# Where a split weight is split: the sums of the second MLP matrix stored whole and split at their use

## Chip, cores and metric

The kernel runs on one core of one Trainium2 chip. The metric is the device time of one execution in microseconds (us), as the median of several runs. A second source is one profiled execution, whose trace gives every instruction of the five engines (TensorE: PE, with its weight loads PEld; VectorE: DVE; ScalarE: ACT; GpSimd: POOL; SyncE: SP, which issues nearly all DMAs here).

## The reference, cut to what matters

One layer of a hybrid decoder over 2048 prompt positions and 8 x 4 sampled ones, in float32, with D_MODEL 1024 and D_FF 4096. Two mixers (a gated linear recurrence and a chunked state-space scan) read one projection, and an MLP follows:

```python
x = x + jnp.concatenate([y_lru, y_ssd], axis=-1) @ w_out
m = rmsnorm(x, g_mlp)
x = x + jnp.square(jax.nn.relu(m @ w_up)) @ w_down
```

`w_up` is 1024 x 4096 and is called the first matrix here, `w_down` is 4096 x 1024 and is called the second.

## The kernel before

**Split products.** The matmuls take operands of the type float32r. Each operand is split into a high part (a copy into float32r, by ACT) and a low part (the operand minus its high part, by DVE), and each product is three matmuls: high x high, high x low, low x high. In the mixers `mm3` (L233 to L235) does that with weights that `load_w` loads (L218) and splits (ACT L220, DVE L222). In the MLP `product` (L832) does it for one block product.

**Fewer block products.** The MLP multiplies 2 x 2 blocks with seven products instead of eight (a Strassen-like scheme). For that it needs sums and differences of weight blocks: seven for each pair of blocks. They depend on the weights alone, so they are prepared once, while the mixers run, by 64 jobs. Job by job the steps are: `job_load` (eight loads of 64 KB, L1128), `job_first` and `job_second` (four DVE additions, L1133 to L1139), `job_higher` (the ACT copy into high parts, tile jh, L1143), `job_lower` and `job_store` (two DVE subtractions, L1146, and two stores to DRAM, of the high parts, L1150, and of the low parts, L1155). The function `tick` is called at set points of the mixers and runs the next step when enough "time" has been counted. Half of the 64 jobs are for the first matrix (they fill the tensors `up0` to `up15`), half for the second (`dn0` to `dn31`). The tiles jt and jh have one buffer each.

**The MLP.** `mlp` goes over three token parts (348, 346 and 346 columns in each half of the token block) and, in each, over eight slices of D_FF (`NQ`). A slice has two `up` phases, of seven products with four pairs of operands each (12 matmuls), and one `down` phase: four groups of output blocks (g), with seven products of two pairs (6 matmuls) each. In the code a weight load of the first matrix serves one product, one of the second serves two (the fourth load of a group serves one). A weight tile `mw` of 128 x 1024 holds high and low parts; there are six. DVE adds each down product from PSUM into the output tiles x2 (or into a sum u), L951, and ACT and DVE prepare operands and splits (L839 and L840, tiles mhh, mhl, ahh, ahl). At the start five weight loads of the first matrix are issued ahead of the token loads (`ahead`).

**What sets the order.** The framework arranges the instructions of each engine at build time, so that the order on an engine isn't quite that of the code; at run time each engine takes its instructions in the order built, and waits for a semaphore where one isn't ready. A DMA waits on SyncE until its target buffer is free.

Of the kernel before, what the change touches and what calls it, by code (L numbers as in the profile page):

```python
# [16 lines left out]
D = 1024  # L17
# [17 lines left out]
MLP = [(0, 348), (696, 346), (1388, 346)]  # L35
MH, FQ = 348, 4
# [3 lines left out]
TF = (1.0, 1.0, 1.05)  # L40
# [2 lines left out]
X2N = ("m", "y", "xdt", "xdd", "hT")  # L43
XTN = ("xdt", "xdd", "hT")
HS, HR = 2, 4


@with_exitstack
def hymba_step(ctx: ExitStack, tc: tile.TileContext,
# [6 lines left out]
    nc = tc.nc  # L56
    V, S, G, T = nc.vector, nc.scalar, nc.gpsimd, nc.tensor
# [94 lines left out]
    r0 = col["cw_s"]  # L152
# [72 lines left out]
    def mm3(ps, w, m, ops, P, b):  # L225

        h, lo = w
        c0, n = P.blocks[b]
        if isinstance(ops[0], list):
            ops, c0 = ops[b], 0  # L230
        nk = len(ops)
        for k, (xh, xl) in enumerate(ops):
            T.matmul(ps[:m, :n], h[:, k, :m], xh[:, c0:c0 + n], start=k == 0, stop=False)  # L233
            T.matmul(ps[:m, :n], h[:, k, :m], xl[:, c0:c0 + n], start=False, stop=False)  # L234
            T.matmul(ps[:m, :n], lo[:, k, :m], xh[:, c0:c0 + n], start=False, stop=k == nk - 1)  # L235

    gwi = [0]
# [566 lines left out]
    def mlp(residual):  # L804
# [6 lines left out]
        ahead = []  # L811

        def bank():
            return ps8.tile([128, 512], F32, tag="mb", name="mb")

        def tmp(name):
            return mp.tile([128, MH], F32, tag="t", name=name, bufs=16)

        def weights(src, op, m):
            if src is up_d[0] and ahead:  # L820
                return ahead.pop(0)
            w = mp.tile([128, 2, 512], F32R, tag="mw", name="mw", bufs=6)
            nc.sync.dma_start(w[:, :, :m].bitcast(F32), src[:, op])
            return w

        def product(ps, w, ops, n, start):

            nk = len(ops)
            for k, (xh, xl) in enumerate(ops):
                c = slice(128 * k, 128 * k + 128)  # L830
                for i, (wi, x) in enumerate(((0, xh), (0, xl), (1, xh))):
                    T.matmul(ps[:, :n], w[:, wi, c], x[:, :n], start=start and k == 0 and i == 0,  # L832
                             stop=k == nk - 1 and i == 2, skip_group_check=not start)

        def halves(t, n, tag, bufs):
# [66 lines left out]

        def up(q, u, mh, n, fill=()):

            src = up_d[2 * q + u]
            x, y, z, w = bank(), bank(), bank(), bank()
            product(x, weights(src, 0, 512), mh[0], n, True)
            after(0, fill)
            p1 = tmp("p1")
            S.activation(p1[:, :n], x[:, :n], AF.Copy)  # L910
            product(y, weights(src, 1, 512), mh[1], n, True)
            after(1, fill)
            v = tmp("v")
            V.tensor_sub(v[:, :n], p1[:, :n], y[:, :n])
            product(z, weights(src, 2, 512), mh[2], n, True)
            after(2, fill)
            p5 = tmp("p5")
            S.activation(p5[:, :n], z[:, :n], AF.Copy)
            product(w, weights(src, 3, 512), mh[3], n, True)
# [4 lines left out]
            product(x, weights(src, 4, 512), mh[4], n, False)  # L924
            after(4, fill)
            c11 = tmp("c11")
            S.activation(c11[:, :n], x[:, :n], AF.Relu)
            product(z, weights(src, 5, 512), mh[5], n, False)
# [3 lines left out]
            product(w, weights(src, 6, 512), mh[6], n, False)  # L932
            after(6, fill)
            c21 = tmp("c21")
            V.tensor_sub(c21[:, :n], w[:, :n], v[:, :n])
            for c in (c22, c12, c21):
                S.activation(c[:, :n], c[:, :n], AF.Relu)  # L937
            for c in (c11, c12, c21, c22):
                S.activation(c[:, :n], c[:, :n], AF.Square)
            return operands((c11, c12, c21, c22), n, "ah", 29)  # L940

        def down(q, act, x2, us, c0, n, steps):
            for g in range(4):
                if steps:
                    steps.pop(0)()
                src = dn_d[4 * q + g]
                hi, lo = x2[g], x2[g + 4]
                c11, c12, c21, c22 = hi[:, :n], hi[:, n:2 * n], lo[:, :n], lo[:, n:2 * n]

                def add(c, ps, op=ALU.add):  # L950
                    V.tensor_tensor(out=c, in0=c, in1=ps[:, :n], op=op)  # L951

                x, y, z, w = bank(), bank(), bank(), bank()
                ws = {}

                def prod(i, ps, start):
                    if i % 2 == 0:
                        t = mp.tile([128, 2, 512], F32R, tag="mw", name="mw", bufs=6)
                        m = min(2, 7 - i)
                        tv = t.rearrange("p a (b c) -> p (a b c)", c=256)[:, :m * 512]  # L960
                        nc.sync.dma_start(tv.bitcast(F32).rearrange("p (o c) -> p o c", c=512),
                                          src[:, i:i + m].rearrange("p o h c -> p o (h c)"))
                        ws[0] = t.rearrange("p a (b c) -> p a b c", c=256)
                    product(ps, ws[0][:, i % 2], [a[i] for a in act], n, start)
# [12 lines left out]
                prod(2, z, True)  # L977
                add(c22, z, ALU.subtract)
                prod(3, w, True)
                add(c22, w)  # L980
                prod(4, x, False)
                add(c11, x)
                prod(5, z, False)
                add(c12, z)
                prod(6, w, False)
                add(c21, w)
                if q == NQ - 1:
                    V.tensor_add(c12, c12, u)
                    V.tensor_sub(c21, c21, u)
                    V.tensor_sub(c22, c22, u)  # L990
# [120 lines left out]
    dn_d = [dr.tile([128, 7, 2, 256], F32, name=f"dn{j}") for j in range(4 * NQ)]  # L1111
    jobs = []
    for q in range(NQ):
        for u in range(2):
            for k in range(2):
                jobs.append((w_up, FF, 256 * k, 512, [128 * (FQ * q + u + 2 * i) for i in range(2)],
                             up_d[2 * q + u][:, :, :, 256 * k:256 * k + 256]))
        for g in range(4):
            jobs.append((w_down, D, 128 * FQ * q, 256, [128 * (g + 4 * i) for i in range(2)], dn_d[4 * q + g][:, :, :, :]))
    jt, jh = {}, {}  # L1120
    clock = [0, 0.0, 0]
    def job_load(j):

        src, ld, r0, dr_, cols, _ = jobs[j]
        t = jt[j] = wp.tile([128, 7, 256], F32, tag="jt", name="jt", bufs=1)
        for at, i, r in ((0, 0, 0), (3, 1, 0), (4, 0, 1), (6, 1, 1)):
            for k in range(2):
                nc.sync.dma_start(t[:, at, 128 * k:128 * k + 128],  # L1128
                                  dap(src, (r0 + dr_ * r + 128 * k) * ld + cols[i], [[ld, 128], [1, 128]]))
# [6 lines left out]
    def job_second(j):  # L1136
        t = jt[j]
        V.tensor_add(t[:, 1], t[:, 2], t[:, 0])
        V.tensor_add(t[:, 5], t[:, 4], t[:, 1])  # L1139

    def job_higher(j):
        h = jh[j] = wp.tile([128, 7, 256], F32R, tag="jh", name="jh", bufs=1)
# [226 lines left out]
```

## Time and profile before

| | |
|---|---|
| runs, median (lowest to highest of 3) | 3085.63 us (3080.34 to 3088.36) |
| the profiled execution | 3082.9 us, span 3081.2 us |
| mean granted TensorE clock | 0.97 |
| mixers | 0 to about 1724 us |
| MLP | about 1724 to 3081 us |
| DMA: moved, mean rate | 708.99 MB, 230 GB/s |
| last job step of the second matrix | DVE L1146 at 1682.0 us, store L1155 at 1683.0 us |

Rows of groups give line, engine, operation, what it writes and reads, the count, then busy us and mean ns of one, then the idle time of the engine before them and who ended it. A row of a wait gives who waited, for whom, us in total, times and the longest. A row of a timeline gives start, length and, in square brackets, the idle time before it and who ended it. A row of the chain that ended last gives start, length and what ran, or which DMA was on its way.

### The profile page before, as it was taken

The numbers are of one execution on the slowest core, as the hardware profiler recorded it, in microseconds if no ns is written. First come the engines' busy times: TensorE is split into PE (matmuls) and PEld (weight loads), VectorE is DVE, ScalarE is ACT, GpSimd is POOL, SyncE is SP. The second block draws the span as 40 slices with busy tenths as digits, with TensorE's granted clock in tenths as the row PEclk, the third lists the DMA queues.
The fourth block names the chain that finished last, engine by engine and source line by source line (L and its number), as shares of the span: only waits on it lengthen the run. The fifth ranks groups of instructions, "written<-read, shape, count | busy, mean of one in ns | idle before, by whom it ended". The sixth has DMA issues, their size and how long they took to land.

```text
span 3081.2 us, 49470 instructions
## 1 busy us (share of the span) xinstructions
PE 2888.0 (94%) x18150; PEld 2789.5 (91%) x18150; DVE 2168.8 (70%) x4422; ACT 1390.9 (45%) x2580; POOL 171.1 (6%) x270
## 2 busy tenths in 40 slices
PE   6999998989999898899989699999999999999997
PEld 6999897888988887899989599999999999999997
DVE  6888788688777878888787645556845556654556
ACT  5553685354357845444883323233432223432322
POOL 0000120010001300000120000000000000000000
PEclk9999998999999998999999799999999999999999
DMA  5555556766665577666656888888988888988885
GB/s 177 156 186 162 165 178 198 236 199 185 205 192 177 179 239 228 184 195 189 194 183 222 277 289 267 281 277 272 319 280 271 284 267 280 318 265 281 268 276 202
DMA packets 534481, 708.99 MB, mean 230 GB/s; under 512 B 44421, under 2 KB 414265, under 8 KB 534240
## 3 DMA queue, kind: packets, MB, share of 16 engines
q1 hardware_dynamic: 534016, 705.56, 71.8%
q8 instruction: 144, 2.36, 0.3%
q0 software_dynamic: 224, 0.27, 0.1%
q14 instruction: 97, 0.79, 0.1%
HBM read 541.43 MB, written 164.27 MB: 229 GB/s over the span
## 4 chain that ended last, share of the span: by engine, by line
PE 47%; DVE 8%; DMA 5%; ACT 4%; issue 1%; SPq 1%; POOL 0%; DVEq 0%; ACTq 0%
PE mb L832 39%; PE mm L235 2%; PE mm L233 2%; PE mm L234 2%; DVE jt L1146 1%; SPq L1128 1%; DMA dn<-jt 1%; DMA up<-jt 1%; DMA mb<-mn_d 1%; DMA mw<-dn 1%; DMA m<-cum 1%; DVE u L412 1%; DVE yt L1027 1%; DVE th L794 0%; ACT jh L1143 0%
## 5 line engine op out<-in xcount | busy, mean ns | idle before, releaser
L233 PE MATMUL mm<-xh,wh 128*128 128x384 f32 (+3 forms) x2160 | 712.6, 331 | 31.8 <-ACT xe L399 14.5
L235 PE MATMUL mm<-xh,wl 128*128 128x384 f32 (+3 forms) x2160 | 705.8, 328 | 3.9 <-DVE wl L222 3.8
L234 PE MATMUL mm<-xl,wh 128*128 128x384 f32 (+3 forms) x2160 | 705.4, 327 | 0.1
L832 PE MATMUL mb<-mhh,mw 128*128 128x346 f32 (+1 forms) x2688 | 655.2, 323 | 17.2 <-ACT mhh L839 16.6
L832 PE MATMUL mb<-ahh,mw 128*128 128x346 f32 (+1 forms) x2688 | 652.5, 323 | 13.1 <-DVE x L951 4.4
L832 PEld LDWEIGHTS mb<-mhh,mw 128*128 128x128 f32 x2688 | 475.8, 191 | 19.4 <-ACT mhh L839 18.3
L832 PEld LDWEIGHTS mb<-ahh,mw 128*128 128x128 f32 x2688 | 470.7, 189 | 19.6 <-ACT ahh L839 5.7
L233 PEld LDWEIGHTS mm<-xh,wh 128*128 128x128 f32 (+1 forms) x2160 | 409.0, 190 | 47.4 <-ACT xe L399 17.5
L832 PE MATMUL mb<-mhl,mw 128*128 128x346 f32 (+1 forms) x1344 | 437.3, 326 | 1.4 <-DVE mhl L840 1.4
L832 PE MATMUL mb<-ahl,mw 128*128 128x346 f32 (+1 forms) x1344 | 434.1, 323 | 0.4 <-DVE ahl L840 0.2
L235 PEld LDWEIGHTS mm<-xh,wl 128*128 128x128 f32 (+1 forms) x2160 | 408.2, 189 | 13.0 <-DVE wl L222 6.5
L234 PEld LDWEIGHTS mm<-xl,wh 128*128 128x128 f32 (+1 forms) x2160 | 409.0, 189 | 3.8 <-issue 1.0
L951 DVE TENSOR_TENSOR x<-x,mb 128x346 f32<-128x346 f32 (+1 forms) x480 | 244.5, 514 | 144.4 <-PE mb L832 143.1
L220 ACT ACTIVATE wh<-raw 128x1024 fp32r<-128x1024 f32 (+1 forms) x159 | 165.4, 1042 | 241.0 <-PE mm L234 181.0
L832 PEld LDWEIGHTS mb<-mhl,mw 128*128 128x128 f32 x1344 | 255.0, 190 | 2.8 <-DVE mhl L840 2.6
L832 PEld LDWEIGHTS mb<-ahl,mw 128*128 128x128 f32 x1344 | 253.7, 189 | 1.4 <-DVE ahl L840 1.4
L910 ACT ACTIVATE p<-mb 128x346 f32<-128x346 f32 (+1 forms) x48 | 21.9, 457 | 473.0 <-PE mb L832 470.9
L222 DVE TENSOR_TENSOR wl<-raw,wh 128x1024 fp32r<-128x1024 f32 (+1 forms) x159 | 190.7, 1201 | 20.5 <-ACT wh L220 19.4
L412 DVE SCALAR_TENSOR_TENSOR u<-xe,prm,u 128x768 f32<-128x768 f32 (+2 forms) x180 | 169.9, 944 | 16.6 <-ACT u L410 14.6
L233 PE MATMUL mm<-nh,wh 128*128 128x384 f32 (+2 forms) x384 | 131.2, 342 | 30.8 <-DVE x L446 27.8
L937 ACT ACTIVATE c<-c 128x346 f32<-128x346 f32 (+1 forms) x144 | 71.3, 495 | 192.5 <-DVE c L923 114.6
L1146 DVE TENSOR_TENSOR jt<-jt,jh 128x1024 fp32r<-128x1024 f32 (+1 forms) x128 | 137.9, 1094 | 25.0 <-ACT jh L1143 24.8
(305 smaller groups left out, 4218.6 us busy)
## 6 DMA issues: line engine op xcount, KB each, us to landing
mw<-up SPq DMA_DIRECT2D x336, 512.0 KB
mw<-dn SPq DMA_DIRECT2D x288, 512.0 KB
raw<-in_w_in_dram SPq DMA_DIRECT2D x108, 512.0 KB
up<-jh SPq DMA_DIRECT2D x32, 896.0 KB
up<-jt SPq DMA_DIRECT2D x32, 896.0 KB
dn<-jh SPq DMA_DIRECT2D x32, 896.0 KB
dn<-jt SPq DMA_DIRECT2D x32, 896.0 KB
raw<-in_w_out_dram SPq DMA_DIRECT2D x48, 512.0 KB
```

Of the source, the lines that this page charges most:

```text
L220: S.activation(h, raw, AF.Copy)
L222: V.tensor_tensor(out=lo, in0=raw, in1=h.bitcast(F32), op=ALU.subtract)
L233: T.matmul(ps[:m, :n], h[:, k, :m], xh[:, c0:c0 + n], start=k == 0, stop=False)
L234: T.matmul(ps[:m, :n], h[:, k, :m], xl[:, c0:c0 + n], start=False, stop=False)
L235: T.matmul(ps[:m, :n], lo[:, k, :m], xh[:, c0:c0 + n], start=False, stop=k == nk - 1)
L412: V.scalar_tensor_tensor(out=u[:, :W], in0=xe[:, k:k + W], scalar=pc(wn, k * nt + j), in1=u[:, :W], op0=ALU.mult, op1=ALU.add)
L832: T.matmul(ps[:, :n], w[:, wi, c], x[:, :n], start=start and k == 0 and i == 0, stop=k == nk - 1 and i == 2, skip_group_check=not start)
L937: S.activation(c[:, :n], c[:, :n], AF.Relu)
L951: V.tensor_tensor(out=c, in0=c, in1=ps[:, :n], op=op)
L1027: V.scalar_tensor_tensor(out=yt[:m], in0=src[:m], scalar=rs[:m, i:i + 1], in1=gfb[:m, 512 * hf:512 * hf + 512], op0=ALU.mult, op1=ALU.mult)
L1128: nc.sync.dma_start(t[:, at, 128 * k:128 * k + 128], dap(src, (r0 + dr_ * r + 128 * k) * ld + cols[i], [[ld, 128], [1, 128]]))
L1146: V.tensor_tensor(out=jt[j][:, a:b].bitcast(F32R), in0=jt[j][:, a:b], in1=jh[j][:, a:b].bitcast(F32), op=ALU.subtract)
```

## The change

The jobs of the second matrix end after the sums: one step, `job_whole`, stores the seven sums whole (128 x 1792 float32), and the split moves into the MLP. There a load of the second matrix brings sums of two products (128 x 512, or 128 x 256) into a tile `mr` of two buffers (`NR`), ACT copies the high part into `mw`, and DVE subtracts into its second half. `mw` has five buffers instead of six. The loads of both matrices are asked for in the order of their use by `ask`, up to two ahead (`NA`), and `prepare` splits up to two ahead (`NP`). At the start two loads are ahead of the token loads instead of five. In `mm3` the matmuls with low parts of weights come behind all matmuls with high parts. The steps of the jobs are 320 instead of 384, and `tick` counts slower in the same ratio. With `UPJ` false and `DNJ` true the first matrix is still split in the mixers.

```diff
+UPJ, DNJ = False, True
+NR, NM, NA, NP = 2, 5, 2, 2
...
 def mm3(ps, w, m, ops, P, b):
...
             T.matmul(ps[:m, :n], h[:, k, :m], xl[:, c0:c0 + n], start=False, stop=False)
+
+        for k, (xh, xl) in enumerate(ops):
             T.matmul(ps[:m, :n], lo[:, k, :m], xh[:, c0:c0 + n], start=False, stop=k == nk - 1)
...
-        def weights(src, op, m):
-            if src is up_d[0] and ahead:
-                return ahead.pop(0)
-            w = mp.tile([128, 2, 512], F32R, tag="mw", name="mw", bufs=6)
-            nc.sync.dma_start(w[:, :, :m].bitcast(F32), src[:, op])
-            return w
+        def raw_weights(src, m):
+            t = mp.tile([128, 512], F32, tag="mr", name="mr", bufs=NR)
+            nc.sync.dma_start(t[:, :m], src)
+            return t
+
+        def parts_of(t, m):
+            w = mp.tile([128, 2, 512], F32R, tag="mw", name="mw", bufs=NM)
+            S.activation(w[:, 0, :m], t[:, :m], AF.Copy)
+            V.tensor_sub(w[:, 1, :m], t[:, :m], w[:, 0, :m].bitcast(F32))
+            return w
...
+        def ask():
...
+                m = min(2, 7 - i)
+                if DNJ:
+                    asked.append((raw_weights(src[:, i:i + m].rearrange("p o c -> p (o c)"), 256 * m), 256 * m))
...
+        def prepare():
+            if asked:
+                t, m = asked.pop(0)
+                ready.append(parts_of(t, m) if m else t)
+
+        def weights():
+            while len(asked) < NA:
+                n = len(asked)
+                ask()
+                if len(asked) == n:
+                    break
+            while len(ready) < NP and asked:
+                prepare()
+            return ready.pop(0)
...
-        ahead.extend([weights(up_d[0], op, 512) for op in range(5)])
+        while len(asked) < NA:
+            ask()
+        while len(ready) < NP - 1:
+            prepare()
...
+    def job_whole(j):
+
+        nc.sync.dma_start(jobs[j][5], jt[j])
+        del jt[j]
...
-    stages = (job_load, job_first, job_second, job_higher, job_lower, job_store)
+    steps_ = [(st, j) for j in range(len(jobs)) for st in
+              (job_load, job_first, job_second) + ((job_higher, job_lower, job_store) if jobs[j][6] else (job_whole,))]
```

**The order, first place: DVE in a down phase.** The second slice of the first token part, from the end of its first group on. Before, DVE has the last operand split and then only additions from PSUM (u: into the running sum; x: into the output tiles):

```order
L840 TENSOR_TENSOR ahl<-t_18790,ahh 128x348
L951 TENSOR_TENSOR x_18243<-x_18243,mb 128x348 x2
L951 TENSOR_TENSOR x_18247<-x_18247,mb 128x348
L951 TENSOR_TENSOR u<-u,mb 128x348 x2
L951 TENSOR_TENSOR x_18248<-x_18248,mb 128x348 x2
L951 TENSOR_TENSOR x_18244<-x_18244,mb 128x348 x2
L951 TENSOR_TENSOR x_18248<-x_18248,mb 128x348
```

Now, at the same place (L902 is the operand split, L1014 the addition, L830 the new subtraction of a weight):

```order
L902 TENSOR_TENSOR ahl<-t_18685,ahh 128x348
L1014 TENSOR_TENSOR x_18090<-x_18090,mb 128x348
L830 TENSOR_TENSOR mw<-mr,mw 128x512
L1014 TENSOR_TENSOR x_18094<-x_18094,mb 128x348
L1014 TENSOR_TENSOR u<-u,mb 128x348
L830 TENSOR_TENSOR mw<-mr,mw 128x512
L1014 TENSOR_TENSOR u<-u,mb 128x348
L1014 TENSOR_TENSOR x_18095<-x_18095,mb 128x348
L1014 TENSOR_TENSOR x_18091<-x_18091,mb 128x348
L1014 TENSOR_TENSOR x_18095<-x_18095,mb 128x348
L830 TENSOR_TENSOR mw<-mr,mw 128x256
```

The subtractions of loads 5, 6 and 7 of the phase (counted from 0) now stand between the additions, each behind additions that themselves wait for TensorE.

**Second place: PE at the start of the third group of the same phase.** The names are mb (the PSUM bank), ah..h and ah..l (high and low part of an operand) and mw (the weight tile). Before, product by product:

```order
L832 MATMUL mb_18945<-ahh_18635,mw_18949 128x348
L832 MATMUL mb_18945<-ahl_18636,mw_18949 128x348
L832 MATMUL mb_18945<-ahh_18635,mw_18949 128x348
L832 MATMUL mb_18945<-ahh_18795,mw_18949 128x348
L832 MATMUL mb_18945<-ahl_18796,mw_18949 128x348
L832 MATMUL mb_18945<-ahh_18795,mw_18949 128x348
L832 MATMUL mb_18946<-ahh_18639,mw_18949 128x348
```

Now:

```order
L894 MATMUL mb_18864<-ahh_18527,mw_18854 128x348
L894 MATMUL mb_18864<-ahl_18528,mw_18854 128x348
L894 MATMUL mb_18865<-ahh_18531,mw_18854 128x348
L894 MATMUL mb_18865<-ahl_18532,mw_18854 128x348
L894 MATMUL mb_18864<-ahh_18527,mw_18854 128x348
L894 MATMUL mb_18864<-ahh_18690,mw_18854 128x348
L894 MATMUL mb_18864<-ahl_18691,mw_18854 128x348
L894 MATMUL mb_18864<-ahh_18690,mw_18854 128x348
```

The four matmuls that need only the weight's high part, of both products of the load, have moved ahead of the first one that needs the low part (the fifth row).

**Third place: SyncE around the second slice.** Before, loads of `mw` follow each other, each of both parts:

```order
L823 DMA mw<-up_144 128x1024 x7
L823 DMA mw<-up_145 128x1024 x7
L961 DMA mw<-dn_162 128x1024 x3
L961 DMA mw<-dn_162 128x512
L961 DMA mw<-dn_163 128x1024 x3
```

Now the loads of the second matrix go to `mr`, at half the size:

```order
L862 DMA mw<-up_144 128x1024 x7
L862 DMA mw<-up_145 128x1024 x6
L824 DMA mr<-dn_162 128x512
L862 DMA mw<-up_145 128x1024
L824 DMA mr<-dn_162 128x512 x2
L824 DMA mr<-dn_162 128x256
L824 DMA mr<-dn_163 128x512 x3
```

The first load of the phase has moved ahead of the last one of the up phase, and the third waits for a buffer that only a subtraction on DVE frees.

More of the change, by code (lines that the diff above doesn't have):

```diff
@@ new lines, in parts_of, with whole_weights, order @@
+        def parts_of(t, m):
+            w = mp.tile([128, 2, 512], F32R, tag="mw", name="mw", bufs=NM)
+            S.activation(w[:, 0, :m], t[:, :m], AF.Copy)
+            V.tensor_sub(w[:, 1, :m], t[:, :m], w[:, 0, :m].bitcast(F32))
+            return w
+        def whole_weights(src):
+            w = mp.tile([128, 2, 512], F32R, tag="mw", name="mw", bufs=NM)
+            tv = w.rearrange("p a c -> p (a c)")
+            return w, tv
+        def order():
+            for _ in MLP:
+                for q in range(NQ):
+                    for u in range(2):
+                        for op in range(7):
+                            yield ("u", up_d[2 * q + u], op)
+                    for g in range(4):
+                        for i in range(0, 7, 2):
+                            yield ("d", dn_d[4 * q + g], i)
@@ new lines, in mlp @@
+        todo = order()
+        asked, ready = [], []
+        def ask():
+            e = next(todo, None)
+            if e is None:
+                return
+            kind, src, i = e
+            if kind == "u":
+                if UPJ:
+                    asked.append((raw_weights(src[:, i], 512), 512))
+                else:
+                    w, tv = whole_weights(src)
+                    nc.sync.dma_start(w.bitcast(F32), src[:, i])
+                    asked.append((w, 0))
+            else:
+                m = min(2, 7 - i)
+                if DNJ:
+                    asked.append((raw_weights(src[:, i:i + m].rearrange("p o c -> p (o c)"), 256 * m), 256 * m))
+                else:
+                    w, tv = whole_weights(src)
+                    nc.sync.dma_start(tv[:, :m * 512].bitcast(F32).rearrange("p (o c) -> p o c", c=512),
+                                      src[:, i:i + m].rearrange("p o h c -> p o (h c)"))
+                    asked.append((w, 0))
@@ L903, in up, with upw @@
         def up(q, u, mh, n, fill=()):
-            src = up_d[2 * q + u]
+            def upw(t):
+                return lambda wi, k: t[:, wi, 128 * k:128 * k + 128]
             x, y, z, w = bank(), bank(), bank(), bank()
-            product(x, weights(src, 0, 512), mh[0], n, True)
+            product(x, upw(weights()), mh[0], n, True)
             after(0, fill)
@@ L910, in up @@
             S.activation(p1[:, :n], x[:, :n], AF.Copy)
-            product(y, weights(src, 1, 512), mh[1], n, True)
+            product(y, upw(weights()), mh[1], n, True)
             after(1, fill)
@@ L914, in up @@
             V.tensor_sub(v[:, :n], p1[:, :n], y[:, :n])
-            product(z, weights(src, 2, 512), mh[2], n, True)
+            product(z, upw(weights()), mh[2], n, True)
             after(2, fill)
@@ L918, in up @@
             S.activation(p5[:, :n], z[:, :n], AF.Copy)
-            product(w, weights(src, 3, 512), mh[3], n, True)
+            product(w, upw(weights()), mh[3], n, True)
             after(3, fill)
@@ L923, in up @@
             V.tensor_sub(c22[:, :n], c22[:, :n], p5[:, :n])
-            product(x, weights(src, 4, 512), mh[4], n, False)
+            product(x, upw(weights()), mh[4], n, False)
             after(4, fill)
@@ L927, in up @@
             S.activation(c11[:, :n], x[:, :n], AF.Relu)
-            product(z, weights(src, 5, 512), mh[5], n, False)
+            product(z, upw(weights()), mh[5], n, False)
             after(5, fill)
@@ L931, in up @@
             V.tensor_add(c12[:, :n], v[:, :n], z[:, :n])
-            product(w, weights(src, 6, 512), mh[6], n, False)
+            product(w, upw(weights()), mh[6], n, False)
             after(6, fill)
@@ L957, in prod @@
                     if i % 2 == 0:
[L958 to L964, printed above, removed]
+                        ws[0] = weights()
+                    t, h = ws[0], i % 2
+                    if DNJ:
+                        at = lambda wi, k: t[:, wi, 256 * h + 128 * k:256 * h + 128 * k + 128]
+                    else:
+                        at = lambda wi, k: t[:, h, 256 * wi + 128 * k:256 * wi + 128 * k + 128]
+                    product(ps, at, [a[i] for a in act], n, start)
                 if q == 0:
@@ L1110, in hymba_step @@
     up_d = [dr.tile([128, 7, 2, 512], F32, name=f"up{j}") for j in range(2 * NQ)]
-    dn_d = [dr.tile([128, 7, 2, 256], F32, name=f"dn{j}") for j in range(4 * NQ)]
+    dn_d = [dr.tile([128, 7, 256], F32, name=f"dn{j}") for j in range(4 * NQ)]
     jobs = []
@@ L1156, in job_store @@
         del jt[j], jh[j]
-    stages = (job_load, job_first, job_second, job_higher, job_lower, job_store)
+    steps_ = [(st, j) for j in range(len(jobs)) for st in
+              (job_load, job_first, job_second) + ((job_higher, job_lower, job_store) if jobs[j][6] else (job_whole,))]
     def tick(w):
-        n = len(stages)
-        clock[1] += w * TF[clock[2]]
-        while clock[1] >= 1 and clock[0] < n * len(jobs):
+        clock[1] += w * TF[clock[2]] * len(steps_) / 384
+        while clock[1] >= 1 and clock[0] < len(steps_):
             clock[1] -= 1
-            j, st = divmod(clock[0], n)
-            stages[st](j)
+            st, j = steps_[clock[0]]
+            st(j)
             clock[0] += 1
```

13 lines of the change are left out of this document (5 added, 8 removed).

## The prediction

> **What bounds the kernel now.** First the page: span, busy shares and slices.
>
> ```profile
> span 3081.2 us, 49470 instructions
> PE 2888.0 (94%) x18150; PEld 2789.5 (91%) x18150; DVE 2168.8 (70%) x4422; ACT 1390.9 (45%) x2580; POOL 171.1 (6%) x270
> ```
>
> Then busy time by stage: the mixers up to 1724 us, the MLP behind them.
>
> ```profile
> 0.00:1724.00 1724.00, 1567.02 (x9942) 1482.70 (x9942) 1374.73 (x2615) 957.21 (x1573) 166.05 (x269) 0.96 0.63 193
> 1724.00:3081.00 1357.00, 1320.94 (x8208) 1306.75 (x8208) 794.08 (x1807) 433.71 (x1008) 5.04 (x1) 0.99 0.84 278
> ```
>
> The columns are length, PE, PEld, DVE, ACT, POOL, granted clock, DMA share, GB/s. In the MLP PE has 36 us idle of 1357 (97% busy) at clock 0.99, DVE works 59% and ACT 32%. In the mixers PE has 157 us idle, with DVE at 80%. So the MLP is bound by TensorE, and anything that delays it there is paid in full; the mixers are a mesh of PE, DVE, ACT and DMA, where freed work pays in part. Next, what PE waits for, in the MLP (first two rows, from 1740 to 3055 us) and in the mixers.
>
> ```profile
> PE mb L832 <- DVE x L951: 4.4, 2, 2.5
> PE mb L832 <- DMA mw<-dn: 4.3, 4, 1.9
> ...
> PE mm L233 <- DVE x L446: 30.1, 14, 5.3
> PE mm L235 <- DVE wl L222: 8.2, 9, 1.7
> ```
>
> Split weights arrive in time now: 4.3 us of waiting for 384 loads of the second matrix. The queue of SyncE says why: its loads wait for a free buffer, so they are issued as early as six buffers allow.
>
> ```profile
> SPq L961 <- PE mb L832: 498.1, 363, 5.2
> ```
>
> **Mixers: what is removed.** Of 64 jobs 32 lose their split: one ACT copy, two DVE subtractions, and one of two stores.
>
> ```profile
> L1146 DVE TENSOR_TENSOR jt<-jt,jh 128x1024 fp32r<-128x1024 f32 x64 | 78.1, 1220 | 25.0 <-ACT jh L1143 24.8
> L1146 DVE TENSOR_TENSOR jt<-jt,jh 128x768 fp32r<-128x768 f32 x64 | 61.9, 967 | 0.0
> L1143 ACT ACTIVATE jh<-jt 128x1792 fp32r<-128x1792 f32 x64 | 108.6, 1697 | 98.8 <-DVE jt L1139 74.5 <-DMA raw<-in_w_out_dram 22.5 <-issue 1.4
> ```
>
> That is 32 x (1.220 + 0.967) = 70 us of DVE and 32 x 1.697 = 54 us of ACT. What of it lies on the path is told by the chain that ended last; in the mixers it is followed from 1038 to 1724 us (686 us).
>
> ```profile
> by line: PE mm L235 10.1%; PE mm L233 10.0%; PE mm L234 9.8%; issue 4.7%; DVE jt L1146 4.0%; SPq L1128 4.0%; DMA dn<-jt 3.2%; DMA up<-jt 3.1%; DMA m<-cum 2.7%; DVE u L412 2.5%; DVE th L794 2.2%; ACT jh L1143 2.2%; DVE wl L222 1.9%; DVE mn L
> ```
>
> L1146 and L1143 have 6.2% of 686 us = 42.5 us; half belongs to the second matrix, 21 us, and over the whole 1724 us that is 21 x 1724/686 = 53 us. A chain that loses a link is soon replaced by the next one, so the bounds are 0 and -53 us; I take the middle, -27. The dropped store widens the better end: dn<-jt has 3.2% (22 us, 55 scaled), and half of that, 28, may go, so -81. The job steps are fewer (320 instead of 384), but the ticks are stretched in the same ratio and the end of the mixers is not set by them: cost 0.
>
> **Mixers: the low parts of weights last.** In mm3 each low part is used after all high parts, so wl is due two thirds of the product later. PE's 8.2 us for wl should go: -8, bounds 0 (the next input is late instead) and -8.2.
>
> **MLP start.** Two weight loads are issued ahead of the token loads instead of five.
>
> ```profile
> 1716.44 7.15 DMA mb<-mn_d
> ```
>
> The first tokens landed 7.15 us after their issue, behind 2.5 MB of weights. Three loads of 512 KB fewer at 278 GB/s are 5.6 us; the third load is then due behind the tokens, so I take -3 (bounds 0 and -5.6).
>
> **MLP: what is added.** Each of the 24 down phases (3 token parts x 8 slices of FF) uses 16 weight loads: per group of output blocks three with two products and one with one. Each now lands as sums of 512 columns (256 for the fourth), is copied by ACT and then subtracted by DVE. Prices lie between neighbouring sizes:
>
> ```profile
> L951 DVE TENSOR_TENSOR x<-x,mb 128x346 f32<-128x346 f32 x320 | 163.0, 514 | 97.4 <-PE mb L832 96.5 <-DMA mw<-dn 0.4
> L222 DVE TENSOR_TENSOR wl<-raw,wh 128x1024 fp32r<-128x1024 f32 x156 | 189.9, 1218 | 20.5 <-ACT wh L220 19.4
> L839 ACT ACTIVATE ahh<-t 128x346 fp32r<-128x346 f32 x128 | 57.7, 486 | 5.1 <-DVE t L848 5.0
> L220 ACT ACTIVATE wh<-raw 128x1024 fp32r<-128x1024 f32 x156 | 164.5, 1056 | 221.5 <-PE mm L234 174.7 <-issue 24.1 <-DVE jt L1138 7.3
> ```
>
> At 512 columns DVE takes 0.514 + 166/678 x 0.704 = 0.69 us and ACT 0.486 + 166/678 x 0.570 = 0.63; at 256, 0.42 and 0.41. With 288 and 96 loads that is 239 us of DVE and 221 us of ACT. By sums there is room: one down phase now shows
>
> ```profile
> 1812.70:1839.50 26.80, 26.80 (x171) 26.69 (x170) 18.25 (x38) 3.42 (x8) 0.00 (x0) 1.00 0.84 273
> ```
>
> 18.25 us of DVE in 26.8, and some 8 us more still fit (four splits are made ahead, in the up phase). The cost comes from order and latency. The raw tiles have two buffers, so a load is issued only when DVE has subtracted the load two before it. This is DVE now, at the start of a down phase:
>
> ```profile
> 1812.77 0.52 DVE L935 TENSOR_TENSOR c<-mb,v 128x348 f32<-128x348 f32 x1 [1.17 <-PE mb L832]
> ...
> 1819.32 0.93 DVE L951 TENSOR_TENSOR x<-x,mb 128x348 f32<-128x348 f32 x2
> 1820.65 0.52 DVE L951 TENSOR_TENSOR x<-x,mb 128x348 f32<-128x348 f32 x1 [0.40 <-PE mb L832]
> ...
> 1823.34 0.52 DVE L951 TENSOR_TENSOR x<-x,mb 128x348 f32<-128x348 f32 x1 [0.44 <-PE mb L832]
> 1824.30 0.52 DVE L951 TENSOR_TENSOR x<-x,mb 128x348 f32<-128x348 f32 x1 [0.44 <-PE mb L832]
> ```
>
> Seventeen operations run back to back from 1812.77 to 1820.25, 0.44 us each (a backlog of the up phase); after that one addition comes with each product, 0.955 us apart. So a group of seven products takes 6.67 us, and load 14 (third of the last group) is due at 3 x 6.67 + 4 x 0.955 = 23.8 us; TensorE does its four high-part products first, so the low part is due at 24.5. In the new order the splits of loads 4, 5 and 6 stand inside the backlog; 19 other operations and three subtractions (0.65 as pitch) end at 19 x 0.44 + 3 x 0.65 = 10.3 us. From load 6 to load 14 the same buffer turns four times. One turn is landing time L + copy 0.63 + subtraction 0.69 + about 0.1 of hand-offs + half an addition in DVE's way, 0.25: L + 1.7. So TensorE is late by 10.3 + 4(L + 1.7) - 24.5 = 4L - 7.4 us in each phase.
>
> L, for 256 KB from issue, stands in no row. The neighbours, sizes first, then the chain's pieces with start and length:
>
> ```profile
> raw<-in_w_out_dram SPq DMA_DIRECT2D x48, 512.0 KB
> gwr<-in_w_a_dram SPq DMA_DIRECT2D x48, 16.0 KB
> ...
> 1528.34 1.91 DMA gwr<-in_w_a_dram
> 1143.46 3.31 DMA raw<-in_w_out_dram
> 1237.98 4.16 DMA raw<-in_w_in_dram
> 2207.32 6.33 DMA mw<-dn
> ```
>
> 16 KB took 1.91 us, 512 KB 3.31 to 4.16 in the mixers and 6.33 in the MLP, where six deep loads queue. With two loads outstanding and half the bytes the quiet rows are nearest: between 1.91 and 3.31, 256 KB gives 2.6. Then 4 x 2.6 - 7.4 = 3.0 us, times 24 = 72 us. Upper end, L = 3.3: 5.8 x 24 = 139. Lower end: the order pins the split of a group's first load behind the last addition of the group before (0.05 + 0.43 + 0.69 = 1.17 us after the due time, 0.64 of it covered by high-part products) at two group boundaries, 1.06 x 24 = 25 us however fast loads land. Behind the waiting subtraction DVE holds the additions, and TensorE needs those before it can reuse a bank, so nothing overtakes. Up weights now have five buffers instead of six and queue behind the raw loads on SyncE; their cover is four products of 1.9 us. At the two seams between token parts, where PE already waits 4.3 us, I add +4 (bounds 0 and +13).
>
> **Sum.** 3082.9 us is the profiled execution (span 3081.2); 72 + 4 - 3 - 8 - 27 = +38, so 3121 us. The median of the runs, 3085.6, is 0.1% above the profiled one, and I leave it at that.
>
> **Rivals.** (1) The loads hide, and the kernel gets faster: L at or under 2.1 us, so only the pinned 25 us remain: 3082.9 + 25 + 4 - 3 - 8 - 27 = 3074, and with the mixers at -53, 3048. For it: the down phases move half the bytes, and 1.91 us has been seen for a small load. Against it: no 512 KB load in the quieter mixers is under 3.31. The Trainium skill, "DMA: Bandwidth & Descriptors", section "Latency and other measured facts", says that the fixed cost of a DMA shrinks with lighter HBM load; by that rule this rival gains, and in direction the rows agree (3.31 us at share 0.63, 6.33 at 0.84), but how far it goes in a down phase no run here shows. Chance 0.30. (2) Both stages cancel: mixers -53, MLP +60: 3082.9 + 60 + 4 - 3 - 8 - 53 = 3083. Chance 0.12. (3) DVE's order costs more, or L reaches 3.3: 3082.9 + 139 + 4 - 3 - 8 - 27 = 3188; from L = 3.0 it is above 3159. For it: 6.33 us for mw<-dn. Against: that was with six loads in flight. Chance 0.13. (4) The forecast, 3095 to 3160: 0.45.
>
> **Numbers.** A measurement here tells 0.3% (9 us) from no change. Faster is rival 1, 0.30; same rival 2, 0.12; slower the forecast and rival 3, 0.58. The range 3060 to 3175 leaves out about the lowest third of rival 1 (0.10) and half of rival 3 (0.07), under 2 in 10; the forecast's own range is 3095 to 3160.
>
> **What the profile after would show.** Mixers end 20 to 60 us before 1724; no wait of L235 for wl. In the MLP: the wait of SyncE's raw loads turns from PE to DVE; PE waits for ACT's and DVE's mw in the last two groups of each down phase, 2 to 4 us per phase; DVE rises to about 1030 us, ACT to 650, DMA share falls. If PE shows under 1 us per phase, L was too long here; if the raw loads land in over 3 us, rival 3. The prediction is wrong as a whole if the mixers give back more than 60 us, since I only scaled a chain that covers 686 us.

## The result, and the profile after

The changed kernel takes 3181.97 us (median of 4 runs, 3171.44 to 3189.9) against 3086.84 us for the kernel before (median of 4): ratio 1.031, 95% interval 1.0274 to 1.0346. Forecast was 3121 us, with a range of 3060 to 3175; the result lies above it. The direction was right; the loss is 95 us where +38 had been worked out.

The profiled execution took 3189.9 us, 107 us more than the one of before. First the page's span and busy shares, then busy time by stage, cut where the MLP's first matmul starts (columns as in the prediction: length, PE, PEld, DVE, ACT, POOL, clock, DMA share, GB/s):

```profile
span 3188.1 us, 50598 instructions
PE 2950.9 (93%) x18150; PEld 2797.6 (88%) x18150; DVE 2327.1 (73%) x4742; ACT 1544.9 (48%) x2932; POOL 150.6 (5%) x270
```

```profile
0.00:1670.00 1670.00, 1553.59 (x9942) 1473.76 (x9942) 1316.29 (x2551) 908.90 (x1541) 144.78 (x269) 0.97 0.59 180
1670.00:3188.00 1518.00, 1397.35 (x8208) 1323.80 (x8208) 1010.79 (x2191) 635.97 (x1392) 5.84 (x1) 0.97 0.59 191
```

The mixers are 54 us shorter (1724 to 1670), the MLP 161 us longer (1357 to 1518), and 161 - 54 = 107. Both moved the way that was forecast, and both by more. PE's busy time in the MLP rose too, from 1321 to 1397 us for the same 8208 matmuls; the last section comes back to that.

What TensorE waits for, first in the mixers with the MLP's start (0 to 1735 us), then in the MLP (1690 to 3125 us), and last SyncE's own queue in the MLP:

```profile
PE mm L236 <- DVE x L451: 17.8, 15, 2.7
PE mb L894 <- ACT mhh L901: 11.6, 2, 11.0
PE mm L240 <- DVE wl L225: 0.8, 1, 0.8
```

```profile
PE mb L894 <- ACT mw L829: 41.8, 58, 2.0
PE mb L894 <- DVE u L1014: 22.5, 16, 2.5
PE mb L894 <- DVE mw L830: 9.7, 12, 2.2
```

```profile
SPq L824 <- DVE mw L830: 452.9, 286, 12.0
```

The wait for wl fell from 8.2 to 0.8 us and the longest one at the MLP's start from 14.6 (before: `PE mb L832 <- ACT mhh L839: 15.1, 2, 14.6`) to 11.0. SyncE's loads of the second matrix no longer wait for PE but for DVE's subtraction, as forecast; TensorE waits for split weights, and, which was not priced, for an addition (u, L1014).

**Where the 161 us sit.** From the starts of the matmuls in both traces: the two up phases of a slice kept their length (26.9 us together). The 18 down phases away from seams and ends went from 26.7 to 33.3 us each: 18 x 6.6 = 119 us. The two seams between token parts (from the start of a part's last down phase to the end of the next part's first up phases) went from 68.7 and 70.1 to 79.2 and 79.6, 20 us; the end grew by 10, the first pair of up phases by 2.4, and the first down phases of the three parts by 9. One ordinary down phase (the second slice of the second token part) by quarters, 42 of its 168 matmuls each, before and after:

```profile
2260.20:2266.93 6.73, 6.73 (x44) 6.62 (x43) 6.53 (x16) 3.54 (x9) 0.00 (x0) 1.00 0.69 203
2266.93:2273.60 6.67, 6.67 (x44) 6.67 (x43) 4.43 (x10) 0.00 (x0) 0.00 (x0) 1.00 0.86 279
2273.60:2280.23 6.63, 6.63 (x45) 6.63 (x43) 3.61 (x7) 0.00 (x0) 0.00 (x0) 1.00 0.90 331
2280.23:2286.86 6.63, 6.63 (x45) 6.63 (x44) 3.61 (x7) 0.00 (x0) 0.00 (x0) 1.00 0.88 282
```

```profile
2256.40:2267.99 11.59, 9.49 (x45) 8.18 (x43) 9.03 (x19) 7.16 (x17) 0.00 (x0) 0.85 0.34 109
2267.99:2275.62 7.63, 6.98 (x45) 6.54 (x43) 6.76 (x16) 1.37 (x4) 0.00 (x0) 1.00 0.23 71
2275.62:2284.09 8.47, 7.36 (x43) 6.57 (x43) 5.93 (x12) 2.20 (x4) 0.00 (x0) 1.00 0.35 108
2284.09:2291.37 7.28, 7.21 (x43) 6.71 (x44) 5.27 (x10) 1.68 (x3) 0.00 (x0) 1.00 0.70 228
```

In this phase the first quarter alone loses 4.9 us, the other three 3.5. Over the 18 phases, the time by which each matmul starts later than 0.16 us behind the one before gives 3.1 us for the first quarter and 0.3, 1.4 and 1.6 for the others: 6.4 us per phase.

**What holds the first quarter.** The chain that ended last, from 2253.60 to 2263 us (the load that it begins with set out earlier); the phase starts at 2256.40:

```profile
2247.87 5.81 DMA mr<-dn
...
2253.70 0.64 ACT mw L829
...
2254.36 0.70 DVE mw L830
...
2255.09 2.70 DMA mr<-dn
...
2257.81 0.64 ACT mw L829
...
2258.47 0.70 DVE mw L830
...
2259.19 2.72 DMA mr<-dn
...
2262.02 0.64 ACT mw L829
...
2262.71 0.58 PE mb L894
```

This is the turn of a raw buffer, two times over: copy, subtraction, load, copy. One turn takes 2257.81 - 2253.70 = 4.11 us, the next 4.21, of which the load is 2.70 and 2.72. It brings two loads, since there are two buffers. The copies shown are those of loads 0, 2 and 4 of the phase. TensorE's order wants load 4 early: while the phase's operands are still being made, its first product stands between those of loads 0 to 3, at place 19 of 168 (counted from 0; so it does in all 18 phases, in the kernel before too). From the order of the changed kernel at that place (mw_23973 is load 0, mw_24058 load 2, mw_24096 load 4):

```
L894 MATMUL mb_24033<-ahh_23858,mw_24058 128x346
L894 MATMUL mb_24033<-ahl_23859,mw_24058 128x346
L894 MATMUL mb_24033<-ahh_23858,mw_24058 128x346
L894 MATMUL mb_24034<-ahh_24009,mw_23973 128x346
L894 MATMUL mb_24106<-ahh_23842,mw_24096 128x346
```

Nineteen matmuls at 0.16 us are 3.0 us, so load 4 is due at 2259.4; its high part is there at 2262.66. Over the 18 phases it is there 5.1 us into the phase at the mean (3.1 to 6.5), 2.1 us after it is due. In the same place ACT and DVE, which take their work in order, hold the operands back behind splits that aren't ready. Here ACT's copy of load 2 waits for its load, DVE's subtraction for that copy, and TensorE, at place 15, for the addition u behind it (over the 18 phases this place has 1.0 us of the quarter's 3.1):

```profile
2257.81 0.63 ACT L829 ACTIVATE mw<-mr 128x512 fp32r<-128x512 f32 x1 [0.78 <-DMA mr<-dn]
```

```profile
2258.47 1.11 DVE L830 TENSOR_TENSOR mw<-mr,mw 128x512 fp32r<-128x512 f32 x2 [0.46 <-ACT mw L829]
...
2260.36 0.51 DVE L1014 TENSOR_TENSOR u<-u,mb 128x346 f32<-128x346 f32 x1
```

```profile
2261.01 0.39 PE L894 MATMUL mb<-ahh,mw 128*128 128x346 f32 x1 [1.36 <-DVE u L1014]
...
2262.71 0.58 PE L894 MATMUL mb<-ahh,mw 128*128 128x346 f32 x1 [0.40 <-ACT mw L829]
```

### The profile page after: what moved, and what is told of

Its sections match the earlier page's. It is cut to its first block, busy times and chain, and to the rows that moved or that the text cites. A ratio compares the mean times of both kernels' runs of the same rounds, so it can differ in the third digit from the quotient of the medians.

```text
span 3188.1 us, 50598 instructions
## 1 busy us (share of the span) xinstructions
PE 2950.9 (93%) x18150; PEld 2797.6 (88%) x18150; DVE 2327.1 (73%) x4742; ACT 1544.9 (48%) x2932; POOL 150.6 (5%) x270
## 4 chain that ended last, share of the span: by engine, by line
PE 58%; DMA 16%; DVE 14%; ACT 8%; issue 3%; SPq 1%; ACTq 0%; DVEq 0%
PE mb L894 24%; DMA mr<-dn 11%; PE mm L236 9%; PE mm L237 9%; PE mm L240 9%; ACT mw L829 3%; DVE mw L830 2%; DMA m<-cum 1%; PE ax L723 1%; DVE x L1014 1%; PE ax L719 1%; DVE u L417 1%; DVE th L799 1%; PE ax L695 1%; SPq L1194 1%
## 5 line engine op out<-in xcount | busy, mean ns | idle before, releaser
L894 PE MATMUL mb<-ahh,mw 128*128 128x346 f32 (+1 forms) x2688 | 704.8, 338 | 93.2 <-ACT mw L829 43.5
L236 PE MATMUL mm<-xh,wh 128*128 128x384 f32 (+3 forms) x2160 | 692.8, 331 | 28.4 <-ACT xe L404 13.7
L237 PE MATMUL mm<-xl,wh 128*128 128x384 f32 (+3 forms) x2160 | 688.7, 329 | 1.5 <-DVE xl L381 1.1
L894 PE MATMUL mb<-mhh,mw 128*128 128x346 f32 (+1 forms) x2688 | 656.3, 324 | 11.7 <-ACT mhh L901 11.6
L894 PEld LDWEIGHTS mb<-ahh,mw 128*128 128x128 f32 x2688 | 478.6, 194 | 155.8 <-ACT mw L829 71.1
L894 PEld LDWEIGHTS mb<-mhh,mw 128*128 128x128 f32 x2688 | 477.6, 191 | 13.7 <-ACT mhh L901 12.4
L829 ACT ACTIVATE mw<-mr 128x512 fp32r<-128x512 f32 (+1 forms) x384 | 220.0, 576 | 521.2 <-DMA mr<-dn 441.5
L894 PE MATMUL mb<-mhl,mw 128*128 128x346 f32 (+1 forms) x1344 | 438.9, 327 | 2.5 <-DVE mhl L902 2.1
L894 PE MATMUL mb<-ahl,mw 128*128 128x346 f32 (+1 forms) x1344 | 434.1, 329 | 3.3 <-DVE ahl L902 2.5
L240 PE MATMUL mm<-xh,wl 128*128 128x384 f32 (+4 forms) x2160 | 396.3, 323 | 0.0
L240 PEld LDWEIGHTS mm<-xh,wl 128*128 128x128 f32 (+1 forms) x2160 | 350.5, 187 | 4.5 <-issue 0.9
L830 DVE TENSOR_TENSOR mw<-mr,mw 128x512 fp32r<-128x512 f32 (+1 forms) x384 | 239.1, 623 | 122.1 <-ACT mw L829 116.3
L1014 DVE TENSOR_TENSOR x<-x,mb 128x346 f32<-128x346 f32 (+1 forms) x480 | 243.8, 513 | 74.0 <-PE mb L894 66.1
L894 PEld LDWEIGHTS mb<-ahl,mw 128*128 128x128 f32 x1344 | 259.7, 194 | 8.0 <-DVE ahl L902 7.3
L894 PEld LDWEIGHTS mb<-mhl,mw 128*128 128x128 f32 x1344 | 255.7, 190 | 5.1 <-DVE mhl L902 4.8
L450 DVE TENSOR_TENSOR mm<-mm,bc 128x384 f32<-128x384 f32 (+2 forms) x144 | 74.7, 523 | 69.3 <-PE mm L240 68.8
```

Of the source, the lines that this page charges most:

```text
L450: V.tensor_mul(ps[:, :n], ps[:, :n], bc[:, c0:c0 + n])
L829: S.activation(w[:, 0, :m], t[:, :m], AF.Copy)
L830: V.tensor_sub(w[:, 1, :m], t[:, :m], w[:, 0, :m].bitcast(F32))
L894: T.matmul(ps[:, :n], w(wi, k), x[:, :n], start=start and k == 0 and i == 0, stop=k == nk - 1 and i == 2, skip_group_check=not start)
```

## The experiments

They ran four at a time, each four on one chip beside runs of the kernel before (medians 3081.6, 3080.1 and 3081.2 us there); ratios are to those. "Down phase" is the mean of the same 18 phases, from the starts of the matmuls in the run's trace.

| kernel | us | ratio (95%) | first MLP matmul | MLP | down phase |
|---|---|---|---|---|---|
| before (first profile) | 3086.8 | 1 | 1724.2 | 1357 | 26.7 |
| changed (first profile) | 3182.0 | 1.031 (1.0274-1.0346) | 1670.1 | 1518 | 33.3 |
| e1_stored | 3095.2 | 1.0038 (1.002-1.0055) | 1710.5 | 1384 | 27.4 |
| e2_idle_work | 3109.4 | 1.0083 (1.0065-1.0102) | 1712.1 | 1396 | 27.9 |
| e3_four_raw | 3053.2 | 0.9907 (0.9888-0.9926) | 1673.4 | 1383 | 26.9 |
| e4_in_place | 3068.5 | 0.9952 (0.9932-0.9971) | 1676.3 | 1396 | 27.7 |
| e5_three_raw | 3041.4 | 0.9874 (0.9856-0.9892) | 1657.9 | 1382 | 26.9 |
| e6_old_mm3 | 3160.9 | 1.0265 (1.024-1.029) | 1663.9 | 1492 | 32.0 |
| e7_six_tiles | 3066.2 | 0.9953 (0.9936-0.9969) | 1703.4 | 1357 | 26.7 |
| e8_pool_split | 3215.4 | one run | 1667.0 | 1547 | 32.1 |
| e9_three_six | 3051.0 | 0.9902 (0.9887-0.9916) | 1663.7 | 1385 | 26.9 |
| e10_three_six_old | 3051.5 | 0.9906 (0.9891-0.9921) | 1661.2 | 1389 | 26.8 |
| e11_two_six | 3146.8 | 1.0218 (1.0203-1.0233) | 1664.5 | 1484 | 31.3 |
| e12_changed | 3164.7 | 1.0283 (1.0264-1.0302) | 1660.9 | 1498 | 32.6 |

**The split back in the mixers (e1_stored).**

```diff
-UPJ, DNJ = False, True
+UPJ, DNJ = False, False
...
-    dn_d = [dr.tile([128, 7, 256], F32, name=f"dn{j}") for j in range(4 * NQ)]
+    dn_d = [dr.tile([128, 7, 2, 256], F32, name=f"dn{j}") for j in range(4 * NQ)]
...
-... dn_d[4 * q + g][:, :, :], False))
+... dn_d[4 * q + g][:, :, :, :], True))
```

> The second matrix is split and stored in the mixers again, as before; the order of mm3, the five weight buffers and the two loads ahead stay as in the changed kernel. Theory A (all of the loss in the MLP comes from splitting there): the down phases return to 26.7 us each, the MLP to 1357-1361 us; the mixers keep only what mm3's order and the start give, 8 to 20 of the 54 us: 3065 to 3078 us in all. Rival B (the loss comes from five buffers and loads asked two ahead): the down phases stay at 30 us or more, over 3130 us. Rival C (mm3's order gave most of the 54 us in the mixers): the first MLP matmul still stands near 1670, and the whole is about 3030 us.

Measured 3095 us, between A and B: nearly all of the phases' loss goes (33.3 to 27.4 us), but the MLP still takes 27 us more than before, and TensorE now waits for the loads themselves:

```profile
PE mb L894 <- DMA mw<-dn: 15.4, 20, 2.4
```

Rival C is out: the mixers give back 54 us with the shorter jobs and 14 without. So the split in the MLP and something else in the change both cost.

**One weight tile more (e7_six_tiles).**

```diff
-NR, NM, NA, NP = 2, 5, 2, 2      (of e1_stored)
+NR, NM, NA, NP = 2, 6, 2, 2
```

> The kernel of e1_stored (no split in the MLP) with six weight tiles instead of five. e1_stored's MLP took 1384 us against 1357 before: 0.7 us in each down phase, 4 us at each seam, 2 at the start. Theory H (one weight tile less): MLP 1357 to 1362 us, 3070 us in all. Rival I (the loads are asked for in another order, two ahead): MLP stays near 1384 us, 3095 us.

Theory H: the MLP is back at its old length,

```profile
1703.00:3060.00 1357.00, 1322.34 (x8208) 1307.50 (x8208) 792.96 (x1807) 434.11 (x1008) 5.71 (x1) 0.99 0.83 279
```

so without a split the fifth instead of the sixth tile costs 27 us, and the order of asking nothing. At ratio 0.9953 this kernel, which splits everything in the mixers as before, is itself 0.5% faster than the old one.

**The work without the waits (e2_idle_work).**

```diff
             (of e1_stored, at each split)
+            d = mp.tile([128, 512], F32R, tag="mr", name="dw", bufs=NR)
+            S.activation(d[:, :m], gfb[:, :m], AF.Copy)
+            V.tensor_sub(d[:, :m], gfb[:, :m], d[:, :m].bitcast(F32))
```

> The kernel of e1_stored, and at each place where a load of the second matrix would be split ACT copies and DVE subtracts the same number of columns of a constant tile: the same work, which waits for no load and for which nothing waits. Theory A1 (the down phases lose by waits, not by the work): within 10 us of e1_stored, the down phases at most 27.2 us. Rival A2 (the work itself, in the way of the operands' splits at the start of a down phase, costs the 3.1 us of the first group): 24 x 3.1 = 74 us more than e1_stored.

14 us more than e1_stored, 0.4 us per down phase: somewhat more than A1's 10, far from A2's 74. The phases, 27.9 us, are over A1's limit of 27.2, but those of e1_stored itself (27.4) are too. Here the order set at build time could place the work freely, so this prices the engines' time alone, not its place among the operands.

**More raw buffers (e3_four_raw, e5_three_raw).**

```diff
-NR, NM, NA, NP = 2, 5, 2, 2
+NR, NM, NA, NP = 4, 5, 2, 2      (e3: also yt 4 instead of 6, last step k = 2 instead of 3)
+NR, NM, NA, NP = 3, 5, 2, 2      (e5: also ah 28 instead of 29)
```

> The changed kernel with four raw buffers instead of two (the output tiles yt have four instead of six for the room, and the last step takes two tiles at a time instead of three, some us at the very end). Theory A1 (the last three groups of a down phase lose 3.3 us to the turn of two raw buffers, the first group 3.1 us to the handover of ACT and DVE from the up phase): the last three groups lose nothing, the first keeps 2 to 3 us: 3182 - 24 x 3.3 = about 3103 us, 3085 to 3120. Rival D (DVE's order, not the landing, holds the later groups): 3170 to 3190 us.

> The changed kernel with three raw buffers (the tiles ah have 28 buffers instead of 29 for the room; the output tiles and the last step are as in the changed kernel). Theory A (everything the down phases lose comes from the turn of the raw buffers; the turn of 4.3 us shared by three gives one load in 1.43 us, under the 1.67 us in which TensorE uses one): the down phases within 0.5 us of 26.9 us, and without e3's changes to the output tiles the seams and the end lose some 10 us less: 3040 to 3055 us. Rival (three are on the edge, the handover to the down phase needs four): 1 to 3 us per phase remain, 3070 to 3115 us.

Both remove the whole loss of the ordinary phases, the first quarter's too (3.1 to 0.1 us), which I had expected to stay in e3. So the first quarter, too, lost by the wait for raw buffers and not by the work in the way. The third buffer does two things. Behind the first loads of a phase, the copies of loads 8 to 15 follow each other every 1.41 us at the mean of the 18 phases, where the changed kernel has 2.02. And loads 0, 1 and 2 are issued 33, 30 and 21 us ahead of the phase, where the changed kernel has 9.7, 8.7 and 2.5; the copy of load 4 is done 0.8 us into each phase. The same four quarters in e5:

```profile
2204.92:2211.76 6.84, 6.84 (x43) 6.65 (x43) 6.63 (x15) 4.94 (x11) 0.00 (x0) 1.00 0.22 66
2211.76:2218.60 6.84, 6.83 (x44) 6.55 (x42) 6.19 (x15) 1.35 (x4) 0.00 (x0) 1.00 0.37 107
2218.60:2225.46 6.86, 6.86 (x42) 6.75 (x43) 6.40 (x13) 2.92 (x5) 0.00 (x0) 1.00 0.50 148
2225.46:2232.12 6.66, 6.66 (x45) 6.66 (x44) 4.73 (x10) 1.05 (x2) 0.00 (x0) 1.00 0.85 272
```

DVE is at 90 to 97% in the first three, and TensorE has no idle time. With 3041 us, e5 is the fastest kernel here, 1.3% under the kernel before (0.9856 to 0.9892), a small gain but clear of the noise. The 25 us by which its MLP still exceeds 1357 lie at the two seams (77.1 and 77.0 us, together 15), the end (4), the first pair of up phases (2), and 0.16 us in each ordinary down phase (3).

**The split in place (e4_in_place).**

```diff
-            t = mp.tile([128, 512], F32, tag="mr", name="mr", bufs=NR)
+            w = mp.tile([128, 2, 512], F32R, tag="mw", name="mw", bufs=NM)
...
-            V.tensor_sub(w[:, 1, :m], t[:, :m], w[:, 0, :m].bitcast(F32))
+            V.tensor_sub(t[:, 1, :m], t[:, 1, :m].bitcast(F32), t[:, 0, :m].bitcast(F32))
```

> The changed kernel without raw buffers: a load lands in the low half of a weight tile, ACT copies it to the high half, DVE subtracts in place; six weight tiles, three loads asked ahead. A buffer now waits for TensorE alone. Theory A1: the last three groups lose nothing, and the first group loses 0 to 3 us (the copies no longer wait for a landing, but stand in the same places): 3182 - 79 - (0 to 70) = 3035 to 3105 us. Rival D (DVE's order holds the later groups): 3150 us or more. Rival E (the split work with its order costs the first group 3.1 us whatever the buffers): 3095 to 3105 us.

3068 us, within A1: with buffers that wait for TensorE alone, 1.0 us per phase remains. D and E are out. It costs no more room than the kernel before, but three raw buffers are better.

**Six tiles and two raw buffers, six and three (e11_two_six, e9_three_six), the changed kernel beside them (e12_changed).**

```diff
-NR, NM, NA, NP = 2, 5, 2, 2
+NR, NM, NA, NP = 2, 6, 2, 2      (e11: also yt 4, last step k = 2)
+NR, NM, NA, NP = 3, 6, 2, 2      (e9: also yt 4, last step k = 2, ah 28)
```

> The changed kernel with two raw buffers still, but six weight tiles (yt four, the last step two tiles at a time). Theory A: the turn of two raw buffers stays, the last three groups of a down phase keep about 3 us; the first group gets back at most the 0.8 us that five tiles cost without a split, and the seams 4 us each: 3145 to 3165 us. Rival L (the sixth tile is what the split lacked): below 3080 us.

> The changed kernel with three raw buffers and six weight tiles (room: ah 28 instead of 29, yt four instead of six, the last step two tiles at a time). Theory A and H together (the split's cost is the turn of two raw buffers, the rest of the MLP's loss is the missing weight tile): down phases at 26.8 us, the MLP at 1357 to 1372 us (the end some 5 us longer by yt), 3015 to 3035 us in all. Rival (with splits in the MLP a sixth tile buys nothing): as e5_three_raw, MLP near 1382 us, 3041 us.

> The changed kernel itself, beside the others on one chip: ratio 1.03 to before, first MLP matmul 1655 to 1672 us, down phases 32 to 33.5 us.

With two raw buffers the sixth tile helps (3165 to 3147 us), but the last three quarters keep 3.4 us: theory A. The first quarter went from 2.5 to 1.0 us, more than the 0.8 that was expected; the seams gave nothing (157.8 us together, then 160.3). The traces say where the first quarter got it: loads 0 and 1 are issued 11.0 and 10.5 us ahead of the phase instead of 9.7 and 8.7, and the copy of load 4 is done 3.9 us into it instead of 4.9. So with two raw buffers the first quarter hangs on two things, the turn and how early the phase's first loads are issued. With three raw buffers the sixth tile buys nothing: e9 is at e5's phases, and its rival was right. e9 is 10 us slower than e5, on another chip and with four output tiles; the longer end (59.0 against 54.8 us from the last down phase on) is 4 of them. So the costs don't add: the tile is worth 27 us to stored halves, 18 us with two raw buffers and nothing with three.

**mm3's order (e6_old_mm3, e10_three_six_old).**

```diff
-
-        for k, (xh, xl) in enumerate(ops):
             T.matmul(ps[:m, :n], lo[:, k, :m], xh[:, c0:c0 + n], start=False, stop=k == nk - 1)
```

> The changed kernel with mm3's old order: each low part of a weight is used right behind its high part. Theory F (mm3's order gave the 10 us by which the mixers of e1_stored end earlier than before): 3182 + 10 = 3192 us, the first MLP matmul near 1680. Rival G (with the shorter jobs the low parts come in time anyway): 3178 to 3186 us, the first MLP matmul near 1670.

> The kernel of e9_three_six with mm3's old order. Rival G of e6 (mm3's order is worth nothing once the jobs are shorter): within 8 us of e9_three_six, first MLP matmul within 8 us. Theory F (it is worth 10 us): 10 us or more slower.

e10 equals e9 (0.9906 and 0.9902): once the jobs are shorter, the order of the low parts is worth nothing. e6 points the same way (1.0265 against e12's 1.0283, on another chip), though its 3161 us are below both forecasts, which set out from the 3182 of the first runs. Its wait for wl is back at 7.8 us, and other waits of PE are shorter (for x 14.3 us instead of 17.8). With the long jobs of e1 and e7 the mixers' last matmul ended 10 and 17 us earlier than in the first profile of before; whether mm3's order did that there was not tried by itself.

**The split on GpSimd (e8_pool_split).**

```diff
-            S.activation(w[:, 0, :m], t[:, :m], AF.Copy)
-            V.tensor_sub(w[:, 1, :m], t[:, :m], w[:, 0, :m].bitcast(F32))
+            G.tensor_copy(w[:, 0, :m], t[:, :m])
+            G.tensor_sub(w[:, 1, :m], t[:, :m], w[:, 0, :m].bitcast(F32))
```

> The changed kernel with both steps of a split in the MLP (copy and subtraction) on GpSimd, which is idle there; two raw buffers as in the changed kernel. The turn gets longer (an addition of 128x768 on GpSimd took 1.54 us, so some 1 us for each step: 2.7 + 2 = 4.7 us for two loads). Theory J (in the first group TensorE loses 3.1 us since ACT's copies, waiting for a landing, stand ahead of the operands' splits): the first group loses under 1 us, the later groups more than now, 4 to 9 us per phase. Rival K (the first group's weights themselves are late): the first group loses 3 us or more again.

Neither: the first quarter loses 2.2 us, the last 2.5, and each pair of up phases is 1.5 us longer (28.4 us), with waits for loads of the first matrix (`PE mb L894 <- DMA mw<-up: 27.2, 21, 3.0`). There is one run of this kernel. The subtraction took 1.29 us at the median (DVE 0.69), the copy 0.61. It doesn't tell J from K; e3 and e5 do.

## Why the prediction was wrong in size

- **Right: the turn, and that it decides.** Forecast were L = 2.6 us, copy 0.63, subtraction 0.69 and a turn of 4.3; the chain shows 2.70 and 2.72 for the load, and of its 107 pieces of raw loads half lie under 2.71; the turns shown take 4.11 and 4.21 us. The medians of the two steps are

```profile
L829 ACT ACTIVATE mw<-mr x384: 398/631/655, 1700.4 to 3159.3; 128x512 fp32r<-128x512 f32 x192
L830 DVE TENSOR_TENSOR mw<-mr,mw x384: 416/691/696, 1701.1 to 3160.2; 128x512 fp32r<-128x512 f32 x192
```

  "4L - 7.4" gives 3.4 us at L = 2.71, and the last three quarters lost 3.3. Rival 1 needed L at or under 2.1 us; at DMA shares of 0.23 to 0.35 the 256 KB load still took 2.7. The Trainium skill, "DMA: Bandwidth & Descriptors", section "Latency and other measured facts", on which rival 1 drew, says that lighter HBM load makes the fixed cost smaller. In these phases it did not go as far as rival 1 needed.
- **Failed: the count began too late.** The working says "From load 6 to load 14 the same buffer turns four times", starts these turns at 10.3 us into the phase, and has no wait of TensorE before that. In the changed kernel the split of load 6 ended at 13.9 us at the mean of the 18 phases; the four turns from there to load 14 took 17.0 us, where 4(L + 1.7) had given 17.2. So 13.9 + 17.0 - 24.5 = 6.4 us late, where 3.0 stood: the turns were right, and the 10.3 was too small by 3.6. In e5, where the first loads come in time, that split does end at 10.5 us. The turn of two buffers rules from load 2 on, and load 4 is due not after a group (6.7 us) but at place 19 of TensorE's order, 3.0 us into the phase. I read the due time from the groups in the code and not from the order, in which this stands before the change too. That quarter lost 3.1 us per phase, the same again as the term that was summed. The opening backlog of DVE was priced only as a delay of load 6's split, not as one of the operands and additions for which TensorE waits.
- **Failed: "Up weights now have five buffers instead of six ... their cover is four products".** The weight tile taken away was priced at 4 us at the seams; without a split it costs 27 us (e1 against e7), and with two raw buffers 18 us (e12 against e11).
- **Rival 3 came near in time by luck.** Its 3188 us stood on L = 3.3 us, and half of the loads on the chain lie under 2.71. Its other half, that DVE's order costs more, is in the chain only as far as an addition waits behind a split that isn't ready; with three raw buffers the same additions and splits cost nothing.
- **Undersized: the ends of the token parts.** The two seams lost 20 us where 10 stood (4, and 3.0 for each one's down phase), the end 10 where its down phase's 3 stood.
- **Undersized on the other side: the mixers.** The last mixer matmul moved from 1709.6 to 1659.2 us, -50 where -8 - 27 stood; the MLP's start wait gave 3.6 (forecast 3). The 32 jobs without a split are worth 37 to 46 us (1699.4 in e1 against 1662.5 in e3; 1692.8 in e7 against 1647.0 in e5 and 1656.1 in e8), over the middle of 27 and under the bound of 53. mm3's -8 should have been 0: its wait went, and with these jobs nothing of it reached the end (e10 against e9). What gave the rest of the 50 was not tried; single profiles of these mixers differ by 18 us, as said below.
- **The sum.** The 21 down phases away from seams and end lost 128 us where 21 x 3.0 = 63 stood, 65 too many; seams 10, end 7 and first pair of up phases 2 too many: the MLP's +161 instead of +76. Mixers and start gave 54 instead of 38. That is 85 - 16 = 69 us too many in the profiled executions, 107 instead of 38.

## What to carry to other kernels

A load that must be copied and subtracted before its buffer comes free turns at landing plus both steps; divide that by the number of buffers and compare it with the time between uses, from the first load of a phase and not from where the pipeline is steady, and see how long ahead of the phase its first loads are issued. Here 4.2 us over two buffers is 2.1 us against one load per 1.67 us and cost 6.4 us per phase; over three it is 1.4 us and cost nothing. Take the due time of each load from the order on the engine that uses it: an order that fetches later work forward to cover a gap also brings later loads' due times forward.

## What the runs showed of the hardware

- **Busy time hides part of a stall.** PE's idle time in the MLP rose from 36 to 121 us, though the MLP lost 161. After a gap the matmuls restart slower: in the changed kernel's MLP there are 106 gaps of over 0.7 us from start to start; at the median the second matmul behind the gap starts 0.26 us behind the first instead of 0.16, and the first lasts 0.43 instead of 0.32. Two rows of PE's timeline behind a shorter gap show the same (0.43 long, the next 0.27 us later):

```profile
2257.64 0.43 PE L894 MATMUL mb<-ahl,mw 128*128 128x346 f32 x1
2257.91 0.48 PE L894 MATMUL mb<-ahh,mw 128*128 128x346 f32 x2
```

  In the first quarter of the changed phase shown above the granted clock was 0.85, in the other three 1.00. The length of a phase with a fixed number of matmuls tells the loss; the idle row tells about half of it.
- **The same mixers end at different times.** In the eight profiles with the changed kernel's mixers as they are (the changed kernel twice, e3, e4, e5, e8, e9 and e11, on several chips), the first MLP matmul stands between 1657.9 and 1676.3 us, a spread of 18 us. Differences of a few us between two single profiles of the mixers say nothing.
- **GpSimd's subtraction** of 128x512 into float32r took 1.29 us, 1.9 times DVE's 0.69; its copy, 0.61, was as fast as ACT's 0.63.
